# Adaptive modulation in the first mixer: products on TensorE's quarters in place of sums on VectorE, ScalarE and GpSimd

## The chip, the cores and the metric

One core of one Trainium2 chip runs the whole program. The metric is the device time of one execution in microseconds; of the kernel before, three runs are shown, with their median. A separate, profiled execution gave the rows below.

## The reference, cut to what matters

Three transformer layers on 512 tokens of width 1024, in fp32. Each layer begins with adaptive modulation: a vector `c` of 1024 values goes through SiLU and is multiplied with a matrix of 1024 x 6144; the result, plus a bias, is cut into six vectors of 1024 (shift, scale and gate for two sublayers).

```python
c_act = jax.nn.silu(c.astype(jnp.float32))
mod = c_act @ ada_w[l].astype(jnp.float32) + ada_b[l].astype(jnp.float32)
sh1, sc1, gt1, sh2, sc2, gt2 = [m[:, None, :] for m in jnp.split(mod, N_MOD, axis=-1)]
hn = rmsnorm(h_res, norm_mix_g[l]) * (1.0 + sc1) + sh1
h_res = h_res + gt1 * hybrid_mixer(hn, ...)
```

The first layer is a mixer (a gated delta rule in 64-token chunks, "gdn", beside an mLSTM) followed by a mixture of experts. Two layers with attention and a dense feed-forward part follow; they have modulation matrices of their own.

## The kernel before, in words

Activations lie with features on the 128 partitions, in eight blocks. A projection multiplies them with weights in three products each (`mm3`, L391): weights and activations are split into a rounded high half and a low half. Weights come in units of 1024 rows x 256 columns, 1 MB, into one of four buffers named `raw` (`_load`, L289, on the queue of SyncE, SP). ScalarE rounds a part of a unit to `whi`, GpSimd (POOL) or VectorE subtracts to get `wlo` (`_split`, L308). The order of units is taken from a dry run of the program; `_loads` (L376) issues the next load, in program order, as soon as a buffer counts as free, and `_ahead` (L358) splits up to two units ahead. `done` (L382) marks a unit as used.

A column of the modulation is a sum over 1024 rows. A unit of `ada` (L457) makes 256 columns. In the form used in the mixer (`eng` given) ScalarE scales four of the eight row blocks in place by their column of `c` (L478), VectorE does the other four with one multiplication and three multiply-adds into `adacc` (L470, through the helpers at L210 and L214), POOL adds the scaled blocks in one add of 512 columns and two of 256 (L205), and TensorE sums `adacc` over the partitions, 128 columns at a time, with a column of ones (tile `pa`). Eight units are a group of 16 blocks of 128 columns; VectorE adds the bias at the end of a group. The mixer makes three groups, 24 units: groups 1 and 2 of `ada0` and group 0 of `ada1`. Group 0 of `ada0` is made before, at the start of the kernel, in `ada_first` (L495): there the eight row blocks are multiplied on TensorE, with `c` copied 32 times as weights (tile `crep`), and the four quarters of 32 columns of the array write four quarters of the partitions of `pada`; a sum over the partitions with the weight 1/(32 x 1024) follows. `ada` is also used for groups 1 and 2 of `ada1` in the first attention layer, and without `eng` for `ada2` in a feed-forward part.

The order of the work around the change is an order of emission. The main chain is a generator: decay matrices and norms, `gdn` (L975) for heads 0 to 3, then for heads 4 to 7, then `mlstm`. In `gdn`, 31 elimination steps on VectorE (tiles `stmp`, `Tm`, from L1050) solve the triangular systems, then results go through DRAM to change their layout (SP's queue), then come products of 64 x 64 blocks and a recurrence of eight steps. At each yield the main chain gives credit in microseconds, and `drive` (L731) spends it on a filler: the remaining projections of the mixer, stored to DRAM through three staging tiles `stg` (`spill_fm`, L1259; `spill_tm`, L1274), and then the first branch of the output. `weave` (L744) puts one step of `ada` into the filler each time 4.2 us of filler have passed; `ada` yields 0.0, so its steps spend no credit. What is left of the filler when the main chain has ended is emitted after it (`drain`). Each engine works through its instructions in the order of emission, SP's queue too. PSUM has eight banks: three `d` for projections, four `c` for the main chain, one `a` for the columns of the modulation.

Of the kernel before, what the change touches and what calls it, by code (L numbers as in the profile page):

```python
# [10 lines left out]
F32 = mybir.dt.float32  # L11
# [4 lines left out]
AF = mybir.ActivationFunctionType  # L16
OP = mybir.AluOpType
# [4 lines left out]
P = 128  # L22
T = 512
D = 1024
KD = 8
# [150 lines left out]
class Build:  # L176
# [280 lines left out]
    def ada(self, w, c, bias, out, groups, eng=None):  # L457

        for g in groups:
            ps = self.ps.tile([P, T], F32, tag="a", bufs=self.ps_a, name="pa")
            pend = None
            for j in range(9):
                if j < 8:
                    u = self.unit((w, 0, KD, 2048 * g + 256 * j, 256), ("raw",))
                    t = u[1]
                    acc = self.gp.tile([P, 256], F32, tag="adacc", bufs=2, name="adacc")
                    if eng is None:
                        self.ts(acc, t[:, 0, :], c[:, 0:1], None, OP.mult)  # L470
                        for k in range(1, KD):
                            if k == 4:
                                yield 0.0
                            self.stt(acc, t[:, k, :], c[:, k:k + 1], acc, OP.mult, OP.add)
                    else:
                        h = KD // 2
                        for k in range(h, KD):
                            self.act(t[:, k, :], t[:, k, :], AF.Copy, scale=c[:, k:k + 1])  # L478
                        self.ts(acc, t[:, 0, :], c[:, 0:1], None, OP.mult)
                        for k in range(1, h):  # L480
                            self.stt(acc, t[:, k, :], c[:, k:k + 1], acc, OP.mult, OP.add)
                        yield 0.0
                        self.tt(t[:, h:h + 2, :], t[:, h:h + 2, :], t[:, h + 2:h + 4, :], OP.add, eng=eng)
                        self.tt(acc, acc, t[:, h, :], OP.add, eng=eng)
                        self.tt(acc, acc, t[:, h + 1, :], OP.add, eng=eng)
                    self.done(u)
                yield 0.0
                if pend is not None:
                    for i in range(2):
                        self.mm(ps[:, 2 * j - 2 + i:2 * j - 1 + i], pend[:, i * P:(i + 1) * P], self.one)  # L490
                pend = acc
            s = slice(16 * g, 16 * g + 16)
            self.tt(out[:, s], ps[:, 0:16], bias[:, s], OP.add)

    def ada_first(self, w, c, bias, out, pool):  # L495

# [2065 lines left out]
    def mixer(self, mod0, mod1, px):  # L2562

        tc, nc, I, gp, dp = self.tc, self.nc, self.I, self.gp, self.dp
        hi, lo = self.h
        md = lambda i: mod0[:, 8 * i:8 * i + 8]
        ada0 = lambda gs: self.ada("ada0", c1, self.vc("ada_b0"), mod0, gs, nc.gpsimd)
        with tc.tile_pool(name="x0", bufs=1, reuse_waits="tile") as x0:
            xT = x0.tile([P, KD, T], F32, name="x0")
            for m in range(0, KD, 2):  # L2570
# [13 lines left out]
            c1, c2 = self.ada_col("c1"), self.ada_col("c2")  # L2584
# [9 lines left out]
            for k in range(KD):  # L2594
                next(first)
                x, a, b = xT[:, k, :], A[:, k:k + 1], md(0)[:, k:k + 1]
# [8 lines left out]
                if k > 2:  # L2605
# [3 lines left out]
        qk_d, v_d, o_d, z_d, oa_d = [dp.tile([P, n, T], F32, name=s) for s, n in  # L2609
                                     (("qk_d", 8), ("v_d", 4), ("o_d", 4), ("z_d", 4), ("oa_d", 4))]  # L2610
        mg_d = dp.tile([P, 16, T], F32, name="mg_d")
        cv_d = dp.tile([P, 6, T], F32, name="cv_d")
        self.marks = set()
        ada = self.chain(ada0((1, 2)), self.ada("ada1", c2, self.vc("ada_b1"), mod1, (0,), nc.gpsimd))
        with tc.tile_pool(name="mb", bufs=1, reuse_waits="tile") as mb:
            with tc.tile_pool(name="ms", bufs=1, reuse_waits="tile") as ms:
                t8 = lambda pool, tag, name: pool.tile([P, 4, T], F32, tag=tag, name=name)
                t4 = lambda pool, tag, name: pool.tile([P, 2, T], F32, tag=tag, name=name)
                qk0, v0 = t8(mb, "A8", "gqk0"), t4(mb, "A4", "gv0")
                cv0 = [qk0[:, j, :] for j in range(4)] + [v0[:, j, :] for j in range(2)]  # L2620
                with tc.tile_pool(name="mq", bufs=1, reuse_waits="tile") as mq:
                    fill = self.drive(self.chain(self.gates(ms, gp, mq), self.mlstm_gates(gp, mq)), self.gdn_proj(0, cv0))
                    self.drain(fill)
                fill = self.weave(self.chain(
                    self.gdn_proj(1, None, cv_d), self.mark("g1"), self.spill_tm("w_in", 1536, 2, z_d),
                    self.spill_fm("w_in", 2080, 8, qk_d, "mconv"), self.spill_tm("w_in", 3104, 2, v_d), self.mark("ml"),
                    self.spill_tm("w_in", 3616, 2, o_d), self.spill_fm("w_in", 4160, 16, mg_d), self.mark("end")), ada, 4.2)
                with tc.tile_pool(name="mx", bufs=1, reuse_waits="tile") as mx:
                    g1 = {}

                    def pre1():
                        self.until(fill, "g1")
                        g1["qk"], g1["v"] = t8(mx, "B8", "gqk1"), t4(mx, "B4", "gv1")
                        self.dma("sync", g1["qk"], cv_d[:, 0:4, :])
                        self.dma("sync", g1["v"], cv_d[:, 4:6, :])
                        yield 0.0
                        yield from self.gdn_pre(g1["qk"], g1["v"])

                    def pre2():
                        self.until(fill, "ml")  # L2640
                        g1["ml"] = [t8(mb, "A8", "mqk0"), t4(mb, "A4", "mqk1"), t4(mb, "A2", "mqk2")]
                        yield from self.mlstm_pre(g1["ml"], qk_d)

                    sh = [P, 2, 4, 4, 64]
                    Yt = lambda pool, tag: lambda: pool.tile(sh, F32, tag=tag, name="Y")
                    Tt = lambda pool, tag: lambda: pool.tile([P, 32, 32], F32, tag=tag, name="Tm")
                    fill = self.drive(self.chain(
                        self.gdn_pre(qk0, v0, self.gdn_decay(0, mx)),
                        self.gdn(0, mx, qk0, v0, Yt(mx, "B8"), Tt(mx, "B4"), z_d, oa_d, pre1())), fill)
                    fill = self.drive(self.gdn(1, mx, g1["qk"], g1["v"], Yt(mb, "A8"), Tt(mb, "A4"), z_d, oa_d, pre2(), self.gdn_decay(1, mx)), fill)  # L2650
            qk = [t[:, j, :] for t in g1["ml"] for j in range(t.shape[1])]
            ph = contextlib.ExitStack()
            oh, ol = [ph.enter_context(tc.tile_pool(name=n, bufs=1, side="right", reuse_waits="tile")).tile([P, 4, T], F32R, name=n)
                      for n in ("mhh", "mhl")]

            ya = []

            def place():
                ya.extend(self.h_tile(m % 2, 4 + m // 2, F32) for m in range(KD))
                yield 0.0  # L2660

            with tc.tile_pool(name="mp", bufs=1, reuse_waits="tile") as mp:
                fill = self.chain(fill, self.branch_in(oa_d, hi, lo), place(), self.branch_a("wa", (hi[:, 0:4], lo[:, 0:4]), ya, mg_d, mp, 2))
                fill = self.drive(self.mlstm(mp, qk, v_d, o_d, oh, ol), fill)
                self.drain(fill)
# [122 lines left out]
```

## Time and profile before

| | |
|---|---|
| median of 3 runs | 2766.24 us (2765.49 to 2769.7) |
| profiled execution | 2763.61 us, span 2761.9 us |
| TensorE busy | 2524.8 us (91%) |
| VectorE, ScalarE, GpSimd busy | 1546.4, 936.0, 961.5 us |
| modulation units in the mixer | 24, from 110 to 553 us of the span |

The names of the engines in the rows are PE (TensorE), PEld (its weight loads), DVE (VectorE), ACT (ScalarE), POOL (GpSimd) and SPq (SyncE's queue). A row of the timeline tells when a run of equal instructions started, how long it lasted, and in brackets how long the engine had been idle before it and what ended that. In `out<-in` the tile that is written stands first; `x4` counts instructions. An fp32 product is recorded as two. PEclk is the granted share of TensorE's full clock of 2.4 GHz.

### The profile page before, as it was taken

The numbers are of one execution on the slowest core, as the hardware profiler recorded it, in microseconds if no ns is written. First come the engines' busy times: TensorE is split into PE (matmuls) and PEld (weight loads), VectorE is DVE, ScalarE is ACT, GpSimd is POOL, SyncE is SP. The second block draws the span as 40 slices with busy tenths as digits, with TensorE's granted clock in tenths as the row PEclk, the third lists the DMA queues.
The fourth block names the chain that finished last, engine by engine and source line by source line (L and its number), as shares of the span: only waits on it lengthen the run. The fifth ranks groups of instructions, "written<-read, shape, count | busy, mean of one in ns | idle before, by whom it ended". The sixth has DMA issues, their size and how long they took to land.

```text
span 2761.9 us, 35101 instructions
## 1 busy us (share of the span) xinstructions
PE 2524.8 (91%) x13640; PEld 1839.8 (67%) x13640; DVE 1546.4 (56%) x2483; ACT 936.0 (34%) x1536; POOL 961.5 (35%) x649
## 2 busy tenths in 40 slices
PE   7777888787969999889999999999999999999999
PEld 4576776565633333556777777878766777888887
DVE  4996595454255655555455388885444345453523
ACT  3424223443221111233344332323332344442422
POOL 1444454422320000243563333434332343344443
PEclk8889998779979999899999999999999999999999
DMA  9356565643289984333455345553231325132321
GB/s 265 99 159 183 157 181 179 194 128 126 95 318 349 344 311 174 107 107 103 139 165 169 107 140 171 193 171 116 74 109 51 95 75 193 62 106 92 107 89 64
DMA packets 336316, 419.06 MB, mean 152 GB/s; under 512 B 37752, under 2 KB 279904, under 8 KB 327824
## 3 DMA queue, kind: packets, MB, share of 16 engines
q1 hardware_dynamic: 317008, 378.13, 42.1%
q10 hardware_dynamic: 14480, 24.23, 2.6%
q0 software_dynamic: 4656, 14.35, 1.6%
q8 instruction: 114, 1.87, 0.3%
q14 instruction: 58, 0.48, 0.1%
HBM read 387.64 MB, written 33.21 MB: 152 GB/s over the span
## 4 chain that ended last, share of the span: by engine, by line
PE 44%; DVE 6%; issue 3%; POOL 2%; ACT 2%; DMA 2%; ACTq 0%; POOLq 0%; DVEq 0%
PE pd L199 35%; DVE adacc L214 2%; PE psc L199 2%; POOL wlo L205 2%; PE tm L199 2%; PE ptot L199 1%; DMA raw<-in_w_up 1%; DVE cv L214 1%; PE pc L199 1%; PE po L199 1%; DVE h L214 1%; PE pz L199 1%; PE pso L199 1%; PE pst L199 1%; PE prr L199 1%
## 5 line engine op out<-in xcount | busy, mean ns | idle before, releaser
L205 POOL TENSOR_TENSOR wlo<-raw,whi 128x1024 fp32r<-128x1024 f32 (+3 forms) x317 | 721.6, 2283 | 1219.2 <-ACT whi L196 1068.1
L199 PE MATMUL pd<-h,whi 128*128 128x512 f32 (+1 forms) x3440 | 1096.0, 401 | 31.7 <-DVE stg L214 6.7
L199 PEld LDWEIGHTS pd<-h,whi 128*128 128x128 f32 x3440 | 646.3, 193 | 188.3 <-issue 28.6
L199 PE MATMUL pd<-h,wlo 128*128 128x512 f32 (+1 forms) x1720 | 673.8, 392 | 21.2 <-POOL wlo L205 21.2
L196 ACT ACTIVATE whi<-raw 128x1024 fp32r<-128x1024 f32 (+3 forms) x319 | 314.0, 994 | 264.4 <-PE pd L199 127.5
L199 PEld LDWEIGHTS pd<-h,wlo 128*128 128x128 f32 x1720 | 330.9, 192 | 93.5 <-POOL wlo L205 25.5
L214 DVE SCALAR_TENSOR_TENSOR adacc<-raw,cs,adacc 128x256 f32<-128x256 f32 x288 | 211.0, 733 | 9.4
L199 PE MATMUL pd<-fyh,whi 128*128 128x512 f32 (+1 forms) x546 | 205.4, 376 | 8.6 <-ACT whi L196 5.2
L214 DVE SCALAR_TENSOR_TENSOR cv<-pd,vec,cv 128x511 f32<-128x511 f32 (+1 forms) x176 | 131.8, 749 | 143.4 <-ACT cv L196 137.9
L199 PE MATMUL pd<-fyh,wlo 128*128 128x512 f32 (+1 forms) x546 | 202.0, 370 | 5.0 <-POOL wlo L205 5.0
L199 PE MATMUL pd<-fyl,whi 128*128 128x512 f32 (+1 forms) x546 | 202.1, 370 | 2.8 <-DVE fyl L205 2.8
L199 PE MATMUL pgB<-gu,xt 128*64 128x512 f32 (+1 forms) x304 | 153.7, 613 | 3.0 <-DVE xt L205 3.0
L199 PE MATMUL pgA<-gu,xt 128*64 128x512 f32 (+1 forms) x304 | 153.7, 613 | 0.0
L214 DVE SCALAR_TENSOR_TENSOR xTl<-pd,mod,xTl 128x512 f32<-128x512 f32 (+1 forms) x73 | 49.4, 683 | 186.1 <-PE pd L199 186.1
L199 PE MATMUL tm<-whi,h 128*128 128x256 f32 x640 | 129.3, 295 | 8.3 <-ACT whi L196 8.0
L214 DVE SCALAR_TENSOR_TENSOR xT<-pb,mod,xT 128x512 f32<-128x512 f32 x128 | 93.6, 748 | 77.2 <-PE pb L199 77.1
L199 PEld LDWEIGHTS pd<-fyh,whi 128*128 128x128 f32 x546 | 105.1, 192 | 39.8 <-ACT whi L196 8.9
L199 PEld LDWEIGHTS pd<-fyh,wlo 128*128 128x128 f32 x546 | 104.9, 192 | 24.3 <-POOL wlo L205 7.3
L199 PEld LDWEIGHTS pd<-fyl,whi 128*128 128x128 f32 x546 | 105.1, 192 | 19.6 <-DVE fyl L205 3.6
L199 PEld LDWEIGHTS tm<-whi,h 128*128 128x128 f32 x640 | 106.2, 199 | 9.6 <-ACT whi L196 8.3
L199 PE MATMUL tm<-wlo,h 128*128 128x256 f32 x320 | 93.3, 292 | 7.7 <-POOL wlo L205 7.6
L196 ACT ACTIVATE cv<-pd,vec 128x512 f32<-128x512 f32 x88 | 68.2, 776 | 94.6 <-PE pd L199 94.0
(563 smaller groups left out, 3404.5 us busy)
## 6 DMA issues: line engine op xcount, KB each, us to landing
raw<-in_ada SPq DMA_DIRECT2D x64, 1024.0 KB, 5.6
raw<-in_w_in SPq DMA_DIRECT2D x54, 1024.0 KB, 5.4
raw<-in_w_up SPq DMA_DIRECT2D x44, 1024.0 KB, 5.0
gu<-in_wg SPq DMA_DIRECT2D x30, 1024.0 KB, 4.8
gu<-in_wu SPq DMA_DIRECT2D x30, 1024.0 KB
dn<-in_wd SPq DMA_DIRECT2D x59, 512.0 KB, 4.7
raw<-in_w_dn SPq DMA_DIRECT2D x16, 1024.0 KB, 5.2
raw<-in_wo SPq DMA_DIRECT2D x12, 1024.0 KB, 5.2
```

Source lines behind the costliest of these rows:

```text
L196: return self.nc.scalar.activation(out, in_, func, **kw)
L199: return self.nc.tensor.matmul(out, lhsT, rhs, start=start, stop=stop)
L205: return (eng or self.nc.vector).tensor_tensor(out, a, b, op=op)
L214: return (eng or self.nc.vector).scalar_tensor_tensor(out, a, s, b, op0=op0, op1=op1)
```

## The change

A new method `ada_mm` makes the 24 units of the mixer. Each row block of a unit is the moving operand of one fp32 product on TensorE; the weights are a column of `c`, broadcast to 32 columns, and the eight blocks go in turn to the four quarters, two to each. ScalarE copies the 128 x 256 result out of a `c` bank of PSUM to `adacc`. The sum over partitions follows one unit later with the weight 1/(32 x 1024), and VectorE multiplies by 1024 and adds the bias at the end of a group. A unit yields once, with 1.2 us of credit, where it yielded twice with none; the weave's step goes from 4.2 to 8.4 us.

```diff
+    def ada_mm(self, w, c, bias, out, groups):
+
+        for g in groups:
+            pcol = self.ps.tile([P, T], F32, tag="a", bufs=self.ps_a, name="pa")
+            pend = None
+            for j in range(9):
+                if j < 8:
+                    u = self.unit((w, 0, KD, 2048 * g + 256 * j, 256), ("raw",))
+                    ps = self.pc("pada")
+                    for k in range(KD):
+                        q = 32 * (k % 4)
+                        self.mm(ps[q:q + 32, 0:256], c[:, k:k + 1].to_broadcast([P, 32]), u[1][:, k, :], k < 4, k >= 4)
+                    self.done(u)
+                if pend is not None:
+                    for i in range(2):
+                        self.mm(pcol[:, 2 * j - 2 + i:2 * j - 1 + i], pend[:, i * P:(i + 1) * P], self.wmean)
+                if j < 8:
+                    pend = self.gp.tile([P, 256], F32, tag="adacc", bufs=2, name="adacc")
+                    self.act(pend, ps[:, 0:256], AF.Copy)
+                    yield 1.2
+            s = slice(16 * g, 16 * g + 16)
+            self.stt(out[:, s], pcol[:, 0:16], float(D), bias[:, s], OP.mult, OP.add)
...
-        ada0 = lambda gs: self.ada("ada0", c1, self.vc("ada_b0"), mod0, gs, nc.gpsimd)
...
-        ada = self.chain(ada0((1, 2)), self.ada("ada1", c2, self.vc("ada_b1"), mod1, (0,), nc.gpsimd))
+        ada = self.chain(self.ada_mm("ada0", c1, self.vc("ada_b0"), mod0, (1, 2)), self.ada_mm("ada1", c2, self.vc("ada_b1"), mod1, (0,)))
...
-                    self.spill_tm("w_in", 3616, 2, o_d), self.spill_fm("w_in", 4160, 16, mg_d), self.mark("end")), ada, 4.2)
+                    self.spill_tm("w_in", 3616, 2, o_d), self.spill_fm("w_in", 4160, 16, mg_d), self.mark("end")), ada, 8.4)
```

## Rows read from the trace of the kernel before

**Rows 1.** Busy time by stretches: stretch in us, then busy us of each engine.

```profile
110.00:223.50 113.50, 82.46 (x549) 69.48 (x549) 104.89 (x148) 44.52 (x74) 55.69 (x36) 0.87 0.52 153
...
314.00:364.00 50.00, 38.08 (x385) 36.91 (x385) 27.89 (x37) 13.66 (x23) 22.06 (x17) 0.86 0.71 178
...
sum 537.00, PE 429.22 PEld 348.23 DVE 359.27 ACT 210.66 POOL 226.76; mean PE 61.32 PEld 49.75 DVE 51.32 ACT 30.09 POOL 32.39
```

**Rows 2.** The same stretches, tile adacc alone: PE, PEld, DVE and POOL.

```profile
110.00:223.50 113.50, 3.10 (x24) 3.38 (x24) 23.32 (x28) 13.23 (x14) 0.87 0.52 153
...
sum 537.00, PE 13.20 PEld 13.66 DVE 61.44 POOL 40.95; mean PE 1.89 PEld 1.95 DVE 8.78 POOL 5.85
```

**Rows 3.** Groups by line and shape, ScalarE and POOL, 100 to 560 us.

```profile
L196 ACT ACTIVATE raw<-raw,cs 128x256 f32<-128x256 f32 x96 | 40.6, 494 | 5.0 <-DVE adacc L210 5.0
...
L205 POOL TENSOR_TENSOR adacc<-adacc,raw 128x256 f32<-128x256 f32 x48 | 40.9, 853 | 55.5 <-DVE adacc L214 52.7
L205 POOL TENSOR_TENSOR raw<-raw 128x512 f32<-128x512 f32 x24 | 34.4, 1435 | 3.4 <-ACT raw L196 3.4
```

**Rows 4.** Waits of POOL and of SP's queue, 100 to 560 us: total, times, longest.

```profile
POOL adacc L205 <- DVE adacc L214: 52.7, 12, 12.0
...
SPq L217 <- POOL adacc L205: 85.1, 19, 15.2
```

**Rows 5.** Timelines of POOL, TensorE and VectorE around 200 us.

```profile
199.97 1.56 POOL L205 TENSOR_TENSOR adacc<-adacc,raw 128x256 f32<-128x256 f32 x2 [11.28 <-DVE adacc L214]
201.49 7.45 POOL L205 TENSOR_TENSOR wlo<-raw,whi 128x1024 fp32r<-128x1024 f32 x3
...
204.04 0.80 PE L199 MATMUL pd<-h,wlo 128*128 128x512 f32 x1 [9.15 <-POOL wlo L205]
...
204.26 2.44 DVE L205 TENSOR_TENSOR Tm<-Tm,stmp 128x220 f32<-128x220 f32 x1
```

**Rows 6.** Timelines of VectorE and TensorE around 135 us.

```profile
131.59 4.41 DVE L214 SCALAR_TENSOR_TENSOR adacc<-raw,cs,adacc 128x256 f32<-128x256 f32 x3
...
139.66 0.69 PE L202 MATMUL ptr<-const_ident,gqk 128*128 128x128 f32 x2 [6.63 <-DVE gqk L214]
```

**Rows 7.** Timelines of SP's queue, ScalarE and TensorE around 320 us.

```profile
320.19 0.37 SPq L217 DMA_DIRECT2D raw<-in_ada  x1
...
325.76 0.60 ACT L196 ACTIVATE stg<-pot 128x512 f32<-128x512 f32 x1 [5.24 <-DMA v_d<-stg]
...
328.75 0.58 PE L199 MATMUL tm<-whi,h 128*128 128x256 f32 x1 [7.00 <-ACT whi L196]
```

**Rows 8.** TensorE's timeline in `ada_first`; then tile pada: ns least, median, most.

```profile
47.02 0.62 PE L199 MATMUL pd<-h,whi 128*128 128x512 f32 x2
47.48 0.40 PE L199 MATMUL pd<-h,wlo 128*128 128x512 f32 x1
47.81 1.07 PE L199 MATMUL pada<-wa,crep 128*32 128x256 f32 x16
...
L199 PEld LDWEIGHTS pada<-wa,crep x128: 106/118/178, 20.7 to 52.0; 128*32 128x32 f32 x128
...
L515 DVE COPY adacc<-pada x8: 417/418/425, 22.7 to 54.2; 128x256 f32<-128x256 f32 x8
```

**Rows 9.** Busy time by stretches, the end of the driven filler: PE first.

```profile
647.00:661.00 14.00, 14.00 (x55) 11.40 (x55) 3.45 (x5) 4.31 (x7) 2.40 (x1) 0.85 0.47 150
```

**Rows 10.** Busy time after a pause; the granted clock is third from last.

```profile
331.00:336.50 5.50, 5.32 (x25) 5.32 (x26) 0.69 (x1) 0.60 (x1) 2.46 (x2) 0.50 0.59 191
```

**Rows 11.** One unit's load on SP's queue and first use; landing times of `raw`.

```profile
201.56 0.37 SPq L217 DMA_DIRECT2D raw<-in_ada  x1
...
212.69 1.69 ACT L196 ACTIVATE raw<-raw,cs 128x256 f32<-128x256 f32 x4
...
DMA to landing us min/median/max: 5.4/5.7/11.2
```

**Rows 12.** Waits of ScalarE, 100 to 560 us.

```profile
ACT stg L196 <- PE pd L199: 40.4, 6, 14.0
```

## The prediction

> **What bounds the kernel now.** I read four views, in this order. First the busy time by stretches of the stage in which the changed columns are made, because the shares of the whole page mix this stage with others. Second, the rows of the changed instructions alone. Third, who waited for them, with the queue of SyncE (SP) among the waiters. Fourth, the timelines around TensorE's longest pauses.
>
> By stretches [rows 1] no engine is full. From 110 to 647 us TensorE is busy for 429.22 of 537.0 us, so it sits idle for 107.8 us. The first stretch, with the 31 elimination steps of the first group of heads, holds 31.0 us of that (113.5 less 82.46), the stretch from 314 us 11.9 us, the other five 64.9 us. In the first stretch VectorE is busy for 104.89 of 113.5 us: it leads there and TensorE waits. So this stage is bound by a chain that changes engine, and TensorE is second to VectorE at its start.
>
> The 24 units of adaptive modulation cost VectorE 61.44 us in the stage, 23.32 of them in the first stretch [rows 2], ScalarE 40.6 us (96 scaled copies) and GpSimd (POOL) 40.9 + 34.4 = 75.3 us (72 adds) [rows 3]. TensorE gives them only the sums over partitions, which stay.
>
> The reader is to see that these units sit in front of work that TensorE needs. POOL waits 52.7 us for VectorE's part of a unit, and SP, which issues the weight loads and the stores in order, waits 85.1 us until POOL's adds give a weight buffer back [rows 4]. At 200 us [rows 5] POOL has waited 11.28 us for VectorE's part, which stands behind elimination steps; three subtractions that make the low halves of projection weights (wlo) wait behind it, and TensorE pauses 9.15 us for the first of these. While POOL catches up, elimination steps take 2.44 us each. At 139.66 us TensorE has waited 6.63 us for a VectorE result with a 4.41 us block of the unit ahead of it [rows 6]. At 320 us SP may load weights only when POOL's adds are done; the store queued behind that load holds a staging buffer, ScalarE waits 5.24 us for it, and TensorE waits 7.00 us for weights that ScalarE has yet to round [rows 7].
>
> **The change part by part.** (1) Products on TensorE. The same products already run at the kernel's start: 16 records (8 fp32 products, four quarters) in 1.07 us at the full clock, and 0.33 us after the start of the product before, where the two before that took 0.46, 0.23 each [rows 8]: the switch to quarters shows as 0.10 us. 24 units x 1.07 = 25.7 us; the 0.10 x 24 = 2 us goes into the range. The weights are now a broadcast column, not a copied tile. If no load were hidden, 16 x 118 ns [rows 8] less 1.07 us would be 0.8 us more a unit, 20 us in all; below that it is nothing. I take nothing, nearest to the row, where loads run beside products.
>
> A rule of the Trainium skill speaks against this part. "TensorEngine Tiling (Array Packing)", Key Properties, says that a change of tiling mode drains TensorE. "TensorE: Matmul & The Clock Gate" puts a lone full-rate product at (398+N)/2.4 ns; worked out from that, as an estimate, a drain costs some 0.16 us, twice a unit 7.7 us in all, and the gain forecast below would shrink by as much. The row, with 0.10 us, decides.
>
> (2) Where the 25.7 us lands. Each unit now gives 1.2 us of credit, 28.8 us in all, so as much filling work (projections) moves out of the driven stage to its end. It is worked off where TensorE is never idle, after the last chain has ended (14.00 of 14.00 us busy) [rows 9]. So the stage itself keeps about its TensorE work, and the tail pays. The price is certain; the gain must come from pauses. The step of the weave goes from two calls per 8.4 us to one: the same pace, priced at nothing, since the units end before the filler in both.
>
> (3) VectorE loses all four operations of a unit and POOL all three. This pays only where TensorE was paused, so the bound is the idle time of each stretch. First stretch: the pauses of 9.15 and 6.63 us go; of the rest of its 31.0 us, which other work also holds, I take a quarter: 20 us in all. From 314 us: the 7.00 us pause and one more of 11.9: 8 us. The other five stretches: their units have free time beside them more often, and I take 10 of 64.9 us. That is 38; below, only the two named pauses (15.8); above, all of the first two stretches and half of the rest (75). After it, the late ones are ScalarE's roundings and POOL's subtractions of weights, which stay.
>
> (4) The clock. The granted clock is 0.50, 1.2 GHz, for 5.32 us of work after the pause at 320 us [rows 10]. Half of it, 2.7 us, comes back with the pause, and I add 1 us each for the pauses at 139 and 200 us: 5 us. Bounds: 0, and 12 if later pauses go too.
>
> (5) ScalarE drops 40.6 us and gains 24 copies out of PSUM. VectorE's copy of the same tile takes 0.42 us [rows 8], so 10 us. Nothing on the path: ScalarE is busy for 210.66 of 537 us of the stage [rows 1]. What covers it is that the sum of a unit is used one unit later. If the cover is gone, the second rival follows. The copy takes one of four PSUM banks that the head chain shares; priced at nothing for the same reason.
>
> (6) Loads. SP's queue is unchanged in what it issues, 1 MB a unit; a buffer comes free when TensorE's products end, rather than POOL's adds. TensorE, in order, now waits itself for a late load. The shortest lead I found is 201.56 us to 212.69 us, 11.1 us, against 5.7 us to land [rows 11]: nothing.
>
> Sum: 25.7 - 38 - 5 = -17 us. The profiled execution took 2763.6 us (span 2761.9), so 2746; the median of the runs is 2.6 us above it: 2749 us.
>
> **The rivals.** *Larger gain.* The pauses are coupled: a buffer freed early moves the store, the load and the rounding behind it. With the upper 75 of step 3 and 12 of the clock less 25.7, -61; two thirds of the way there from the forecast is about -46, so 2720 us. For it: SP's 85.1 us, and the 2.44 us elimination steps. The Trainium skill, "SBUF — State Buffer", says that VectorE and GpSimd take a shared port pair as an exclusive lock for a whole instruction; by it most of POOL's 75.3 us would also come back to VectorE. The trace agrees where a step of VectorE lasts 2.44 us beside POOL. Against: the subtractions for wlo stay on POOL and keep blocking, and TensorE needs its 82.46 us in the first stretch anyway.
>
> *Slower: ScalarE waits for TensorE.* The copy stands on ScalarE in order, behind products that TensorE reaches late; roundings of the next weights stand behind it. Today ScalarE waits 40.4 us in 6 pieces for projections, 6.7 us each [rows 12]. If 8 of the 24 copies cost such a wait and all of it reached TensorE, +54 us; with half of it hidden by the weights split ahead, +27: 2749 + 27 = 2776 us. It turns slower once the copies together hold TensorE for 17 us, 0.7 us each. Against: ScalarE already waits so, with weights ahead.
>
> *No change: TensorE sets the pace already.* Then only the 15.8 us of named pauses, the 5 us of clock and some 5 us of others come back, and 25.7 us is paid: 2766 us.
>
> *Not what it says:* loads, with buffers freed by an engine that runs late, come late to TensorE, and the pauses only change their name. Same price as the second rival; it shares its chance.
>
> **How the numbers follow.** Forecast (2732 to 2760) 0.45; larger gain 0.23; no change 0.13; slower, both ways, 0.19. A measurement here can tell about 0.2%, 5.5 us. Faster 0.45 + 0.23 = 0.68, same 0.13, slower 0.19. The range leaves out half of the slower cases and some of the larger gains: 2718 to 2773; it takes in the 20 us of unhidden weight loads. The likeliest case's own range is 2732 to 2760.
>
> **What would show it.** Right: products of 1.0 to 1.1 us per unit, TensorE's busy time up by about 25 us; no pause at the first elimination for wlo; SP no longer waiting for POOL's adds, but a little for TensorE; the elimination ending earlier, and a longer run of projections after the last head chain (14 us now, some 40 then). Wrong: ScalarE's waits for the copied tile in the hundreds of ns per unit or above, TensorE waiting for weights of the modulation, a unit of over 1.5 us, or as much idle time as now in the first two stretches.

## The result, and the profile after

The changed kernel takes 2779.56 us (median of 5 runs, 2775.3 to 2783.93) against 2766.24 us: 1.0055 of the time before, interval 1.0037 to 1.0074, or 15 us slower. The forecast was 2749 us with a range of 2718 to 2773 us: the measured time lies above the range, and on the other side of the kernel before. Ratios below are to the kernel before on the same chip; I turn them into microseconds of 2766 us.

The page's busy times, its first part:

```profile
PE 2539.7 (92%) x14024; PEld 1838.0 (66%) x14024; DVE 1479.1 (53%) x2387; ACT 901.4 (33%) x1460; POOL 887.7 (32%) x577
```

VectorE is busy for 67 us less, POOL for 74 us less, ScalarE for 35 us less, TensorE for 15 us more. The relief of the three engines is all there, and the span is 11.5 us longer. The products' own records (tile `pada`) take 27.95 us of TensorE; its other instructions take 13 us less than before, at a mean granted clock of 0.952 against 0.947. Three groups of rows show where the time went. First the timeline of TensorE around one unit, then the tiles with the first and last start of their instructions: `pQ` is the first TensorE work after each elimination, `mhh` is written four times in the mLSTM, and its last write ends the last head chain.

```profile
154.21 0.28 PE L199 MATMUL tm<-wlo,h 128*128 128x256 f32 x1
154.33 0.28 PE L199 MATMUL tm<-whi,h 128*128 128x256 f32 x1
154.54 1.07 PE L199 MATMUL pada<-raw,cs 128*32 128x256 f32 x16
155.54 0.61 PE L199 MATMUL pa<-wmean,adacc 128*128 128x1 f32 x4
...
L199 PE MATMUL pQ<-Xc,M x256: 236/236/258, 204.7 to 391.6; 32*32 32x32 f32 x128
L196 ACT ACTIVATE mhh<-pht x4: 597/597/598, 515.9 to 615.4; 128x512 fp32r<-128x512 f32 x4
```

The same two tiles in the kernel before:

```profile
L199 PE MATMUL pQ<-Xc,M x256: 191/191/238, 228.4 to 419.3; 32*32 32x32 f32 x128
L196 ACT ACTIVATE mhh<-pht x4: 597/597/598, 557.0 to 647.2; 128x512 fp32r<-128x512 f32 x4
```

A unit costs TensorE 1.07 us, as in [rows 8], with its weights broadcast. The first elimination is over 23.7 us earlier (204.7 against 228.4), and the last head chain 31.8 us earlier (615.4 against 647.2). Up to there the change delivers. The busy times by stretches come next: the two of [rows 1], the whole way to the end of the last chain, then the filler that is left and the merge of the two branches.

```profile
110.00:223.50 113.50, 94.76 (x1004) 75.04 (x1007) 82.82 (x126) 33.60 (x49) 33.31 (x15) 0.88 0.60 175
314.00:364.00 50.00, 45.65 (x482) 41.79 (x482) 44.20 (x63) 9.35 (x13) 19.85 (x10) 0.93 0.67 185
110.00:615.40 505.40, 418.39 (x4387) 327.26 (x4388) 290.17 (x517) 164.11 (x279) 143.88 (x100) 0.89 0.54 162
...
615.40:664.00 48.60, 41.45 (x155) 32.23 (x154) 8.45 (x13) 13.90 (x19) 11.95 (x5) 0.82 0.35 114
664.00:699.30 35.30, 26.56 (x97) 20.30 (x95) 16.81 (x17) 11.33 (x17) 10.51 (x4) 0.85 0.54 179
```

In the kernel before, the merge by the same view:

```profile
661.20:687.10 25.90, 23.30 (x97) 17.57 (x95) 15.85 (x16) 9.65 (x15) 10.55 (x4) 1.00 0.55 183
```

The filler behind the last chain has grown from 14 us [rows 9] to 48.6 us, and the merge from 25.9 to 35.3 us for the same 97 records: 44 us given back where 31.8 had been won. The filler's part is nearly three times the number of records (155 against 55). Of its growth of 34.6 us, 27.5 us are TensorE's work; the other 7.1 us are pauses, for the products no longer run back to back: TensorE is busy for 41.45 of 48.60 us, at a granted clock of 0.82. The merge's 97 records take 3.3 us more at a clock of 0.85 against 1.00, and its pauses grow from 2.6 to 8.7 us. TensorE's and ScalarE's timelines of the filler and of the merge's start say where the pauses come from; the last line is the loads of `oat`:

```profile
635.53 1.52 PE L199 MATMUL pd<-h,whi 128*128 128x512 f32 x2 [5.51 <-ACT h L196]
640.39 1.52 PE L199 MATMUL pd<-h,whi 128*128 128x512 f32 x2 [1.64 <-ACT h L196]
670.97 0.79 PE L199 MATMUL pd<-mhh,whi 128*128 128x512 f32 x1 [4.01 <-DVE h L214]
...
634.85 0.63 ACT L196 ACTIVATE h<-oat 128x512 fp32r<-128x512 f32 x1 [4.19 <-DMA oat<-oa_d]
651.26 0.63 ACT L196 ACTIVATE mg<-mg 128x512 f32<-128x512 f32 x1 [6.22 <-DMA mg<-mg_d]
659.60 0.63 ACT L196 ACTIVATE mg<-mg 128x512 f32<-128x512 f32 x1 [6.24 <-DMA mg<-mg_d]
669.57 0.63 ACT L196 ACTIVATE mg<-mg 128x512 f32<-128x512 f32 x1 [7.87 <-DMA mg<-mg_d]
...
L217 SPq DMA_DIRECT2D oat<-oa_d x4: 319/372/455, 631.1 to 637.0; - x4
```

The same loads in the kernel before:

```profile
L217 SPq DMA_DIRECT2D oat<-oa_d x4: 319/372/446, 589.0 to 596.4; - x4
```

The first branch of the output began before as filler of the mLSTM, with its loads 58 us ahead of the end of the last chain; now they start 16 us behind it. Its inputs (`oat`) and gates (`mg`) come back from DRAM, and for the inputs TensorE has nothing beside them that covers the trip.

The filler is also missing where it was taken from. TensorE's timeline at the end of the first elimination:

```profile
193.06 0.39 PE L199 MATMUL pd<-h,wlo 128*128 128x512 f32 x1
204.65 1.08 PE L199 MATMUL pQ<-Xc,M 32*32 32x32 f32 x21 [11.21 <-DMA Xc<-xd]
```

TensorE has run out of work and waits 11.21 us for a layout change through DRAM. The same place after the second elimination costs 6.5 us (the view of waits has 17.7 us in two, and 1.7 us in two in the kernel before). The pauses of [rows 5, 6] are gone, this one has come. Up to the end of the last chain TensorE now pauses for 87.0 us (505.40 less 418.39) against 107.8 us before; over the whole execution for 234 us against 237. Most of what was won in front has come back behind.

### The profile page after: what moved, and what is told of

It reads as the page before. It is cut to its first block, busy times and chain, and to the rows that moved or that the text cites. A ratio compares the mean times of both kernels' runs of the same rounds, so it can differ in the third digit from the quotient of the medians.

```text
span 2773.4 us, 35588 instructions
## 1 busy us (share of the span) xinstructions
PE 2539.7 (92%) x14024; PEld 1838.0 (66%) x14024; DVE 1479.1 (53%) x2387; ACT 901.4 (33%) x1460; POOL 887.7 (32%) x577
## 4 chain that ended last, share of the span: by engine, by line
PE 42%; DVE 6%; issue 3%; POOL 2%; DMA 2%; ACT 2%; ACTq 0%; POOLq 0%; DVEq 0%
PE pd L199 33%; POOL wlo L205 2%; DVE adacc L214 2%; PE psc L199 2%; PE tm L199 2%; DMA raw<-in_w_dn 1%; PE ptot L199 1%; DMA raw<-in_w_up 1%; DVE h L214 1%; DVE cv L214 1%; PE pc L199 1%; PE po L199 1%; PE pz L199 1%; PE pso L199 1%; PE pst L199 1%
## 5 line engine op out<-in xcount | busy, mean ns | idle before, releaser
L214 DVE SCALAR_TENSOR_TENSOR adacc<-raw,cs,adacc 128x256 f32<-128x256 f32 x216 | 155.5, 720 | 6.9
L199 PEld LDWEIGHTS pd<-fyh,whi 128*128 128x128 f32 x546 | 104.8, 192 | 42.0 <-ACT whi L196 12.1
```

The source lines that it names most:

```text
L199: return self.nc.tensor.matmul(out, lhsT, rhs, start=start, stop=stop)
L214: return (eng or self.nc.vector).scalar_tensor_tensor(out, a, s, b, op0=op0, op1=op1)
```

## The experiments

Two questions: is it the products or the 1.2 us of credit that cost, and what in the relief was worth the time? Four of the kernels ran on one chip: e1_no_credit, e2_old_with_credit, e3_products_twice and e4_copy_on_vector.

**The credit away.**

```diff
-                    yield 1.2
+                    yield 0.0
```

> The changed kernel, but a unit yields 0.0 in place of 1.2 us of credit. Credit theory (the loss is the 28.8 us of filler that the credit pushes behind the last head chain, where it waits for DRAM): the run of projections after the last chain falls from 56 us to 15 or 20, the head chains end 10 to 20 us later than in the changed kernel because the filler now covers TensorE's pauses there, and the total is 2750 to 2764 us. Pace theory (the added 25.7 us of products are simply more work for the engine that sets the pace, wherever they stand): the sum stays, 2774 to 2784 us. ScalarE theory (the copies out of PSUM hold ScalarE and with it the rounding of weights): no change either, 2774 to 2784.

Measured: 0.9935 of the kernel before (0.9911 to 0.9960), 18 us faster; 2751.24 against 2770.24 us on that chip. This is faster than the kernel before and than the changed one. By stretches, up to the end of the last chain, then the filler left, then the merge:

```profile
110.00:626.70 516.70, 452.56 (x4487) 353.85 (x4488) 291.87 (x526) 180.09 (x299) 153.24 (x104) 0.88 0.55 168
626.70:639.70 13.00, 13.00 (x56) 10.64 (x55) 2.76 (x4) 3.29 (x5) 2.40 (x1) 0.93 0.50 162
639.70:668.20 28.50, 24.59 (x97) 18.76 (x95) 16.61 (x17) 10.86 (x17) 10.55 (x4) 0.94 0.50 166
```

The filler left is 13.0 us again, without a pause, and the merge 28.5 us. The chains end 11.4 us later than in the changed kernel (626.7 against 615.4), though two thirds of the 155 records moved in front of that. They filled pauses: up to the end of the last chain TensorE pauses for 64.1 us here (516.70 less 452.56) and for 87.0 us in the changed kernel (two expectations below put the 64.1 us at 71, and the one above puts the filler's 48.6 us at 56). Of the pauses that the credit brings, 22.9 us thus stand in the head chains, 7.1 us in the filler left and 4.8 us in the merge. The pause at the first `pQ` is covered:

```profile
207.79 0.98 PE L199 MATMUL pd<-h,whi 128*128 128x512 f32 x2
208.61 0.40 PE L199 MATMUL pd<-h,wlo 128*128 128x512 f32 x1
210.10 1.86 PE L199 MATMUL pQ<-Xc,M 32*32 32x32 f32 x128 [1.09 <-DMA Xc<-xd]
```

The credit theory holds; the pace theory falls, since the same products gave two times 33 us apart.

**The old sums with the credit.**

```diff
-    def ada(self, w, c, bias, out, groups, eng=None):
+    def ada(self, w, c, bias, out, groups, eng=None, cost=0.0):
...
                             self.stt(acc, t[:, k, :], c[:, k:k + 1], acc, OP.mult, OP.add)
-                        yield 0.0
+                        yield cost
...
-        ada0 = lambda gs: self.ada("ada0", c1, self.vc("ada_b0"), mod0, gs, nc.gpsimd)
+        ada0 = lambda gs: self.ada("ada0", c1, self.vc("ada_b0"), mod0, gs, nc.gpsimd, 1.2)
...
-self.ada("ada1", c2, self.vc("ada_b1"), mod1, (0,), nc.gpsimd)
+self.ada("ada1", c2, self.vc("ada_b1"), mod1, (0,), nc.gpsimd, 1.2)
```

> The kernel before, in which a unit of the mixer charges 1.2 us of credit, and nothing else changes. Credit theory: TensorE does the same work, yet 40 us of projections move behind the last chain; the chains end at most 15 us earlier, and the total is 2780 to 2795 us. Pace theory: TensorE's work is as before, so 2762 to 2770. ScalarE theory: no copies, 2762 to 2770.

Measured: 1.0112 (1.0083 to 1.0142), 31 us slower, without any change in what an engine computes. The same three stretches:

```profile
110.00:639.10 529.10, 400.44 (x4005) 325.20 (x4006) 341.50 (x612) 194.33 (x351) 215.52 (x169) 0.85 0.51 153
639.10:689.20 50.10, 41.90 (x160) 32.56 (x159) 9.06 (x15) 13.90 (x19) 14.64 (x8) 0.84 0.37 121
689.20:721.90 32.70, 26.40 (x97) 19.85 (x95) 16.63 (x17) 11.34 (x17) 10.53 (x4) 0.90 0.59 193
```

The chains end only 8 us earlier than before, for 50.10 us of filler left. The time, 2797 us, is 2 us above what the credit theory allowed, and 27 us or more above the other two. So the four kernels make a table, in ratio to the kernel before:

| | credit 0 | credit 1.2 us a unit | the credit alone |
|---|---|---|---|
| sums on VectorE, ScalarE, POOL | 1 | 1.0112 | +31 us |
| products on TensorE | 0.9935 | 1.0055 | 1.0055/0.9935: +33 us |
| the products alone | -18 us | 1.0055/1.0112: -16 us | |

Each difference is good to 7 to 10 us either way, by the intervals. To within that the two parts add up without touching each other. The row of the products takes in the weave's new step, which no run changed alone.

**The products twice**, with and without credit.

```diff
-                    for k in range(KD):
-                        q = 32 * (k % 4)
-                        self.mm(ps[q:q + 32, 0:256], c[:, k:k + 1].to_broadcast([P, 32]), u[1][:, k, :], k < 4, k >= 4)
+                    for i in range(2 * KD):
+                        k = i % KD
+                        q = 32 * (k % 4)
+                        self.mm(ps[q:q + 32, 0:256], c[:, k:k + 1].to_broadcast([P, 32]), u[1][:, k, :], i < 4, i >= 12)
...
-            self.stt(out[:, s], pcol[:, 0:16], float(D), bias[:, s], OP.mult, OP.add)
+            self.stt(out[:, s], pcol[:, 0:16], float(D) / 2, bias[:, s], OP.mult, OP.add)
```

> The changed kernel with each of the eight products of a unit made twice (and half the factor at the end). Pace theory: another 24 x 1.07 = 26 us, 2800 to 2810 us. Credit theory: part of it falls into TensorE's pauses in the head chains (11.2 and 6.5 us before the second solve, and smaller ones), so 5 to 18 us, 2785 to 2797. ScalarE theory: the copies come later by 1 us each and hold ScalarE longer, 30 us or more, 2810 and above.

> The kernel of e1_no_credit with each of the eight products of a unit made twice. It prices the products where the filler again covers the pauses. If every product is paid in full: 24 x 1.07 = 26 us over e1_no_credit, ratio to the kernel before about 1.003. If TensorE's pauses in the head chains (71 us in all in e1_no_credit) still hide a part, as the 9 us of the doubled products with credit suggest: 5 to 18 us over e1_no_credit, ratio 0.995 to 1.000. If the head chains wait for every product: 30 us or more, ratio above 1.004.

Measured: 1.0087 (1.0058 to 1.0116) with credit, 9 us over the changed kernel; 0.9952 (0.9935 to 0.9969) without, 5 us over e1_no_credit. The further products do run (tile `pada` of e6_twice_no_credit, twice the 384 records; their busy time is 48.85 us against 26.75 us in e1_no_credit). The second line is TensorE's busy time in this kernel up to the end of its last chain, at 634.0 us:

```profile
L199 PE MATMUL pada<-raw,cs x768: 379/379/636, 116.5 to 509.6; 128*32 128x256 f32 x192
...
110.00:634.00 524.00, 467.78 (x4871) 362.66 (x4872) 287.47 (x526) 180.75 (x299) 153.28 (x104) 0.89 0.55 166
```

Of the 22 us of further products, 7 us delay the end of the last chain (634.0 against 626.7 us), 8 us fill pauses (56.2 left of 64.1 us), and for the remaining 7 us the 4103 other records of the stretch take less time, 418.9 us in place of 425.8. Why these are shorter was not tested; the stretch's granted clock is 0.89 against 0.88. Neither price, 5 or 9 us, is clear of nothing by the intervals; that both are below 26 us is.

**The copy on VectorE.**

```diff
-                    self.act(pend, ps[:, 0:256], AF.Copy)
+                    self.nc.vector.tensor_copy(pend, ps[:, 0:256])
```

> The changed kernel with the copy out of PSUM on VectorE in place of ScalarE, one edit. ScalarE theory: the 45.9 us that ScalarE waits for these products are gone from in front of the rounding of weights, 10 us or more faster, 2769 us or less. Credit and pace theories: within 5 us of the changed kernel, 2775 to 2785.

Measured: 1.0043 (1.0023 to 1.0063), within the interval of the changed kernel. The waits have moved, as the two views of waits show, ScalarE in the changed kernel and VectorE in this one:

```profile
ACT adacc L196 <- PE pada L199: 45.9, 15, 9.2
```

```profile
DVE adacc L513 <- PE pada L199: 14.3, 7, 4.5
```

Taking 45.9 us of waiting away from ScalarE brings nothing that stands clear of the noise, where the ScalarE theory wanted 10 us or more. The edit also gives VectorE 24 copies of 0.42 us, 10 us in all, and a gain of a few us could hide behind that. But e1_no_credit, the faster kernel by 33 us, has the longer wait: 83.6 us by the same view. The ScalarE theory falls.

**Back with one of the reliefs at a time**, on e1_no_credit. The results of the added operations are not used; their tile takes turns with `adacc` in its two buffers.

```diff
+                    dead = self.gp.tile([P, 256], F32, tag="adacc", bufs=2, name="dead")
+                    self.ts(dead, u[1][:, 0, :], c[:, 0:1], None, OP.mult)
+                    for k in range(1, 4):
+                        self.stt(dead, u[1][:, k, :], c[:, k:k + 1], dead, OP.mult, OP.add)
                     self.done(u)
```

> The kernel of e1_no_credit, with the four operations that VectorE did for a unit added again on the same weight buffer; their result is not used, so only VectorE's time and the hold on the buffer come back, no wait of TensorE for the sum. If VectorE's time on the chain is the relief: 12 to 23 us over e1_no_credit, ratio 0.998 to 1.002, and the same as e10_dead_vector_elsewhere. If the late release of the buffer, and with it SP's queue, is the relief: the same here, but nothing in e10. If neither (POOL's waits and adds are): within 5 us of e1_no_credit, ratio 0.992 to 0.995.

In the second, both operands `u[1][...]` are `self.consts[0][:, 0:256]`.

> As e9_dead_vector_on_weights, but the four operations read a constant tile, so that the weight buffer is free when the products are done. VectorE's time theory: as e9, 12 to 23 us over e1_no_credit. Buffer theory: within 5 us of e1_no_credit, ratio 0.992 to 0.995.

The third has four additions on POOL instead:

```diff
+                    k0 = self.consts[0][:, 0:256]
+                    self.tt(dead, k0, k0, OP.add, eng=self.nc.gpsimd)
+                    for k in range(3):
+                        self.tt(dead, dead, k0, OP.add, eng=self.nc.gpsimd)
```

> The kernel of e1_no_credit with four dead additions of 128x256 on POOL per unit, on a constant tile (about 3 us of POOL a unit, as the three additions of the kernel before had). They wait for nothing. If POOL's time itself, with its blocking of VectorE, was the relief: 10 to 20 us over e1_no_credit, ratio 0.997 to 1.001. If it was only that POOL waited for VectorE in front of other work: within 5 us, ratio 0.992 to 0.995.

Measured: 0.9987 (0.9974 to 1.0000), 0.9970 (0.9956 to 0.9984) and 0.9986 (0.9971 to 1.0002), or 14, 10 and 14 us over e1_no_credit. VectorE's tile of the second and POOL's of the third:

```profile
L214 DVE SCALAR_TENSOR_TENSOR dead<-const_ident,cs,dead x72: 483/485/2496, 119.8 to 502.7; 128x256 f32<-128x256 f32 x72
```

```profile
L205 POOL TENSOR_TENSOR dead<-dead,const_ident x72: 722/741/1607, 120.9 to 505.5; 128x256 f32<-128x256 f32 x72
```

So four operations a unit on VectorE cost about 10 us and four on POOL about 14 us, each to 8 us or so either way, and the two are not told apart. Nor are they quite what the expectations wanted to price. The added tile takes one of the two buffers from ScalarE's copy, and ScalarE waits for the added operations, in the second and in the third kernel:

```profile
ACT adacc L196 <- DVE dead L214: 22.5, 3, 10.3
```

```profile
ACT adacc L196 <- POOL dead L205: 15.4, 3, 7.4
```

In the first kernel this wait is 12.1 us. The costs do not follow it (14, 10 and 14 us for 12.1, 22.5 and 15.4 us), but no run gave the added tile a buffer of its own, so each price may be too high. POOL's additions stand in front of the subtractions for `wlo`, and beside them VectorE is busy for 1489.5 us against 1473.9 in e1_no_credit, with the same 2387 instructions; how much of the 14 us is the one and how much the other was not separated. The late release of the weight buffer could be worth the 4 us between the first two, but their intervals overlap: open. VectorE's and POOL's prices add up to more than the 18 us by which the products win; that gain is the relief less what the products cost.

**Further along the same line.** Filler moved even further forward:

```diff
-                    yield 1.2
+                    yield -0.6
```

> The changed kernel with a unit that yields -0.6 us: 14.4 us of filler move forward into the head chains, where e1_no_credit moved 28.8. Credit theory: the 13 us of projections behind the last chain shrink to almost nothing and the chains grow by less, since TensorE still pauses for 71 us there: 2 to 10 us under e1_no_credit, ratio 0.990 to 0.993. If the pauses that filler can reach are used up: the chains grow by as much as the tail shrinks, within 3 us of e1_no_credit, ratio 0.993 to 0.995; if filler in front of the chain's products delays it, above that.

Measured: 0.9924 (0.9902 to 0.9946), 3 us below e1_no_credit and not to be told from it. In its trace no filler is left, and the last chain ends at 646.9 us, 20 us later than in e1_no_credit, whose run of filler was 13 us. That execution was 7 us above the median of its kernel, so the two are about equal, and this speaks for the second theory, that the pauses within reach are used up. And the modulation of the first attention layer by products too:

```diff
-self.ada("ada1", c2, self.vc("ada_b1"), mods[1], (1, 2), self.nc.gpsimd)
+self.ada_mm("ada1", c2, self.vc("ada_b1"), mods[1], (1, 2))
...
-                fill = self.weave(fill, fill_extra, 3.9)
+                fill = self.weave(fill, fill_extra, 7.8)
```

> The kernel of e1_no_credit, with the 16 units of the first attention layer also made by products, without credit, one call per 7.8 us of filler. If the relief of VectorE, ScalarE and GpSimd is worth as much per unit there as in the mixer (18 us for 24 units): 12 us under e1_no_credit, ratio about 0.989. If what counts is how much TensorE pauses (27 of 450 us between 1150 and 1600 us, against a fifth of the time in the mixer), the 16 x 1.07 = 17 us of products find little to hide in: 3 to 15 us over e1_no_credit, ratio 0.994 to 0.999.

Measured: 0.9933 (0.9912 to 0.9954): neither theory; 16 units less on three engines and 16 units more on TensorE cancel, to 9 us either way. From 1150 to 1600 us TensorE goes from 423.58 (e1_no_credit) to 433.26 us busy in this kernel:

```profile
1150.00:1600.00 450.00, 433.26 (x2244) 322.95 (x2245) 205.98 (x351) 159.11 (x285) 144.88 (x105) 0.99 0.41 131
```

VectorE has lost 38 us and POOL 48 us there, and it brings no more than the products cost.

## Why the prediction was wrong, point by point

**Step 2 failed.** It put the 28.8 us of credit down as a change of place: the moved filler would run "where TensorE is never idle", and its price was the 25.7 us of products that push it there. I read the 14.00 of 14.00 us of [rows 9] as a property of that stretch. It was a property of the projections then in it. The longer run behind the last chain came as forecast ("some 40 then", 48.6 us measured); what failed is its price. In its old place the moved filler had cost less than half of its time: put back in e1_no_credit, some 28 us of it make the chains end 11.4 us later and fill 22.9 us of pauses, two of them (11.21 and 6.5 us) DRAM trips of the head chains. Behind the last chain it costs its full time, its own DRAM trips stand uncovered (7.1 us), and the merge that follows waits for the same loads. The credit alone costs 31 or 33 us, with the sums as with the products; I had it at nothing beyond the products.

**Step 1** was right in its unit (1.07 us, no dearer for the broadcast weights or for the switch to quarters) and wrong in what a unit costs the time. I paid all 25.7 us. A second set of products costs 5 to 9 us by the medians; that the first costs about as much is inferred. The pauses hide about a third of the second set, and other instructions that take less time make up for another. The timeline above shows 0.09 us for the way into a unit (it starts 0.21 us after the product before it, whose like are 0.12 us apart) and nothing on the way out (`pa` starts 1.00 us after the unit, whose records take 1.07 us). The Trainium skill ("TensorEngine Tiling (Array Packing)", Key Properties) says that a change of tiling mode drains TensorE; the estimate of 0.16 us each way, 7.7 us in all, is more than this trace shows.

**Steps 3 and 4** had the mechanism; their size, 38 + 5 = 43 us, is probably too large. The named pauses did go, and work put back on VectorE or on POOL costs time again. At equal credit the products win 18 or 16 us net, which with 5 to 9 us for the products makes a relief of about 21 to 27 us. The clock's 5 us were, if anything, too few: TensorE's other instructions take 13 us less in the changed kernel and 6.5 us less in e1_no_credit, at mean granted clocks of 0.952 and 0.954 against 0.947. The pauses up to the end of the last chain fall from 107.8 to 64.1 us in e1_no_credit, 43.7 us, but the products themselves fill a part of them, so this is not the relief alone. The sum of -17 us agrees with the kernel without credit; by the inferred price of the products that is luck, two errors that cancel, and no run had the relief without the products.

**Step 5 and its rival**: the copy on ScalarE has no price that shows. It waits 45.9 us for TensorE, 1.9 us a unit and so one of the listed signs of being wrong, yet taking it away changes nothing that can be told from noise. **Step 6**: TensorE, as forecast, does not wait for weights of the modulation. SP's queue still waits for buffers, now 106.8 us for the products (100 to 560 us) against 146.2 us for POOL and VectorE before, far from the "little" I expected; in e1_no_credit it is 122.6 us, and that kernel is 33 us faster than the changed one: the length of these waits says little about the time.

Of the rivals the slower side came true, by none of the mechanisms listed. The ones I named were all on engines; the loss was in the order of emission, which the diff showed in one number. The signs listed for being right nearly all came (1.07 us a unit, no pause for `wlo`, an earlier end of the elimination, a longer run behind the last chain), while the time went the other way: they showed that the relief works, and none of them priced the filler.

## What to carry to other kernels

Where filler is handed out against a budget, a charge for new work is a change of schedule of its own: price it by what the displaced filler had been covering, and by what the work that ends up uncovered waits for, not by how busy the tail looks today. Work that moves onto an engine with spread pauses can cost much less than its own time, but only while those pauses are still reachable in the order of emission. And change the work and its charge in separate runs: here they were worth -18 and +33 us.

## What the runs showed of the hardware that was not expected

Additions on POOL whose result is not used, 24 x 4 of about 0.74 us on a constant tile, cost about 14 us of the kernel's time, and VectorE's busy time rose by 15.6 us with the same number of instructions, although VectorE and not POOL led in the first stretch. Doubled products on the quarters of TensorE, 22 us by their own records, cost 5 to 9 us by the medians on an engine that is busy for nine tenths of the span; about a third of them was made up for by other instructions of TensorE that took less time.
